# A two-layer hybrid block with eight experts on one core: who splits the first projection, products in the router's gaps, and the order of the last weight unit

## The chip, the cores and the metric

The kernel runs on one core of a Trainium2 chip. The time is device microseconds of that core for one execution of the whole program. TensorE (PE in the profile) does the matmuls, VectorE (DVE) and GpSimd (POOL) the element-wise work, ScalarE (ACT) copies, casts and activations, SyncE (SP) issues the transfers. "The clock" below is TensorE's granted clock: 1.00 is 2.4 GHz, 0.50 is 1.2 GHz.

## The reference

256 tokens of width 1024 go through two layers, all in fp32.

```
for l in range(2):
    mix = hybrid_mixer(x, ...)      # gated conv (31 taps) + chunked retention, then w_out
    x = layer_norm(ALPHA * x + mix, ln1_g[l], ln1_b[l])
    if l == 0: f = (silu(x @ w1) * (x @ w3)) @ w2           # dense, 3584 wide
    else:      # router: logits = x @ moe_router, best 2 of 8 experts, softmax of the two
               f = sum over the two experts of gate * swiglu_expert(x)
    x = layer_norm(ALPHA * x + f, ln2_g[l], ln2_b[l])
```

In `hybrid_mixer` the input projection gives two gates of 512 for the convolution (glu), then q and k, v and g of 512 each; q and k are rotated, scored against each other under a decay mask and applied to v; the conv output and the retention output go through w_out together.

## The kernel before

**Three products for one.** A fp32 matrix is held as a high part, which is the value rounded to the matmul's fast fp32 format (`fp32r`), and a low part, value minus high part. `mm3` (L150) then does high·high, high·low and low·high, one line each (L152, L153, L154). The high part is a cast on ScalarE (L107), the low part a subtraction on VectorE or on GpSimd (L108); both are in `parts`. Tiles are named `wh`/`wl` for weights, `xh`/`xl` for x, `gah`/`gal` and `gbh`/`gbl` for the gathered tokens of two experts.

**Weights** come in units of 1 MB (128x2048), in the order in which `plan` lists them, into buffers named `raw`. A unit is split in two halves of 128x1024, "first" and "second". The object `W` is this list: `take` hands out the next half and sees to it that a few more are split beyond it, `ahead(n)` only splits ahead. The place in the program at which `take` or `ahead` is called is the place at which the cast and the subtraction stand in ScalarE's, VectorE's or GpSimd's queue: there is no scheduler, each engine runs its instructions in the order in which the code writes them (`manual_schedule`), and waits at each for what it needs. Which engine subtracts is written in the unit: `gp` for GpSimd, `None` for VectorE.

**Layer 0's start.** `glu(0)` and `glu(1)` make the first two gates; after each, `fill(n)` writes n steps of the convolution into VectorE's queue (a first step on L389, then one fused multiply-add per tap on L393). `FILL[0]` begins with 12, so one step and 11 taps stand behind `glu(0)`. Then `proj()` makes q and k from units 4 and 5, both split by GpSimd.

**Between mixer and experts (layer 1).** `ln_end` normalizes 128 tokens (tile t) in two halves of 512 columns: subtract the mean and scale (L274), then multiply by the reciprocal deviation, which GpSimd computes (`rsqrt`), and add (L280). `turn_x` transposes the result on TensorE (L293), ScalarE copies it to `xf` (L294), `logits` multiplies by the router (L322, eight columns), `choose` finds the two best experts with small VectorE operations and writes `sel`. For tile 1 nothing can be done before its `sel`: five small products with a triangle of ones rank the tokens per expert (`pr`), VectorE forms `rk` and with it the four masks `P` (L743), and `gather` multiplies x by the masks in four groups of 256 columns (`pg`, L752), each split into `gah`, `gal`, `gbh`, `gbl` before the expert's first products (`ac`) can use it. `busy(n)` puts n useless 128x128 products on TensorE: 20 before the ranking, 10 behind it.

**The end.** The last unit of the last expert (`rl`, its halves are quarters 2 and 3 of the down projection) is split by half columns. The down projection's sum `y` has two halves of 512 columns, `ys0` and `ys1` are their high and low parts, `put` (L771) brings them back to token order, and the result is added to `acc`, normalized and sent in four pieces of 128x512.

Of the kernel before, what the change touches and what calls it, by code (L numbers as in the profile page):

```python
# [38 lines left out]
TAPS = (12, 11)  # L39
ASIDE = True  # L40
COLQ, W1Q = 1, 2
WARM, WARM1, WARM2 = 40, 20, 10
MOEP = {1: 0}
LATE = 4

# [27 lines left out]
def tile_hybrid(ctx: ExitStack, tc, xT_in, x_in, ws, wm, cols, lnp, gnp, router, ident_in, rot, mask_in, out):  # L73
# [25 lines left out]
    def half(h):  # L99
        return slice(512 * h, 512 * h + 512)  # L100
# [4 lines left out]
    def parts(hi, lo, src, eng=None):  # L105

        sc.copy(hi, src)  # L107
        (eng or v).tensor_tensor(lo, src, f32(hi), op=ALU.subtract)  # L108

    def split(shape, src, pool, tag, bufs=None, eng=None):  # L110
        p = pair(shape, pool, tag, bufs)
        parts(p[0], p[1], src, eng)
        return p
# [7 lines left out]
    def new_spl():  # L121
        scount[0] += 1
        return pair([128, 1024], spools[(scount[0] - 1) % len(spools)], "w")
# [22 lines left out]
    def plan(src, eng=None, kinds=("first", "second")):  # L146
        unit = src if isinstance(src, Unit) else Unit(src, eng)
        W.items += [(k, unit) for k in kinds]
# [14 lines left out]
    for l in range(DEPTH):  # L163
        b = l * MIXU
        for q in (0, 1, 4, 5, 6, 7, 2, 3, 8, 9):
            if l > 0 and q < 2:
                plan(ws[b + q], kinds=("whole",))
            else:
                plan(Unit(ws[b + q], gp if q >= POOL_GLU else None, 2 if l == 0 and q == 1 else 1))
        for q in (2, 3):  # L170
            plan(ws[b + 10 + q], kinds=("whole",))
        for q in (0, 1):
            plan(Unit(ws[b + 10 + q], gp, at=SPL if (l, q) == (DEPTH - 1, 0) else None))
        if l == 0:
            nf, d2 = DFF // 128, None
            for f in range(nf + LATE):
                if f < nf:
                    u = ws[DEPTH * MIXU + f // 2 * 3 + f % 2]
                    plan(u, kinds=("whole",) if f < 2 else ("first", "second"))
                g = f - 1 if f < nf - LATE + 1 else f - LATE  # L180
                if 0 <= g and not nf - LATE < f < nf:
                    if g % 2 == 0:
                        d2 = Unit(ws[DEPTH * MIXU + g // 2 * 3 + 2])
                    plan(d2, kinds=(("first", "second")[g % 2],))
# [83 lines left out]
    def ln_end(t, x, s, st, gt, aside=False):  # L268

        mv = sm.tile([128, 2], F32, tag="mv", name="mv")  # L270
        v.bn_aggr(mv, st)
        rs = rsqrt([128, 1], mv[:, 1:2])
        for h in range(2):
            v.scalar_tensor_tensor(s[:, half(h)], s[:, half(h)], mv[:, 0:1], gt[:, 0, half(h)],  # L274
                                   op0=ALU.subtract, op1=ALU.mult)
            if aside:
                sc.mul(s[:, half(h)], s[:, half(h)], rs[:, 0:1])
                gp.tensor_tensor(x[:, t, half(h)], s[:, half(h)], gt[:, 1, half(h)], op=ALU.add)
            else:
                v.scalar_tensor_tensor(x[:, t, half(h)], s[:, half(h)], rs[:, 0:1], gt[:, 1, half(h)],  # L280
                                       op0=ALU.mult, op1=ALU.add)
# [3 lines left out]
        nc.sync.dma_start(gt, bass.AP(tensor=lnp.tensor, offset=lnp.offset + i * 2 * D, ap=[[0, 128], [D, 2], [1, D]]))  # L285
        return gt

    def turn_x(t, psum):

        for k in range(0, KD, 4):  # L290
            p = psum.tile([128, 4, 128], F32, tag="wk", name="wk")
            for j in range(4):
                pe.transpose(p[:, j, :], x[:, t, 128 * (k + j):128 * (k + j) + 128], ident)  # L293
            sc.copy(xf[:, k:k + 4, tok(t)], p)  # L294
# [74 lines left out]
    def mixer(l, psum, mp, me, heads, then):  # L369
# [179 lines left out]
        for cc in range(2):  # L549
            glu(cc)  # L550
            if l == 0 and cc == 0:
                for q in range(W1Q, 4):
                    part_w(1, q, r1)
                nc.sync.dma_start(rott, rot)
                nc.sync.dma_start(ident, ident_in)
            fill(next(F))
        if l == 0:
            nc.sync.dma_start(mask, mask_in)
        diags()
        pq = proj()  # L560
# [49 lines left out]
        for t in range(NT):  # L610
            s, st = ln_new(mp, ("PT", "qk")[t])
            if t < NT - 1:
                for k in range(0, 4, 2):
                    for h in range(2):
                        wout_c(t, h, range(k, k + 2))
                for h in range(2):
                    ln_sum(t, h, acc[t][h], x, s, st)
            else:
                for h in range(2):
                    wout_c(t, h)  # L620
                    ln_sum(t, h, acc[t][h], x, s, st)
                turn_x(0, psum)
                if l > 0:
                    pl = bank(psum, [128, NT, NE])
                    logits(pl, 0)
                else:
                    heads = then(psum)
            ln_end(t, x, s, st, gt, ASIDE and l > 0 and t == 0)
        if l > 0:
            choose(0, pl[:, 0, :])  # L630
            parts(xn[0][:, 0, :], xn[1][:, 0, :], x[:, 0, :])
        turn_x(NT - 1, psum)
        if l == 0:
            part_x()
            W.ahead(3)
        else:
            logits(pl, 1)
            parts(xn[0][:, 1, :], xn[1][:, 1, :], x[:, 1, :])
            choose(1, pl[:, 1, :])
        return heads  # L640

# [125 lines left out]
    def put(ys, PT, t, new=None):  # L767

        p = new() if new else ptp.tile([128, 512], F32, tag="tp", name="pc")
        for i in range(2):  # L770
            pe.matmul(p, PT[:, tok(t)], ys[i], start=(i == 0), stop=(i == 1))  # L771
        return p

    def add(p, t, h, g, to=None):
        o = acc[:, t, half(h)]
        v.scalar_tensor_tensor(o if to is None else to, p, g, o, op0=ALU.mult, op1=ALU.add)  # L776
# [47 lines left out]
    def down(hT, q, w, y, first, last, hs=(0, 1)):  # L824
        for h in hs:
            mm3(y[h], two(hT, A, q), two(w, A, half(h)), first and q == 0, last and q == 3)
# [22 lines left out]
            pass  # L849

    g0 = tokens_of(0)
    W.ahead(4)
    cnt = mo.tile([128, 1], F32, name="cnt")
    v.tensor_reduce(cnt, pr[:, 2, :], axis=AX.X, op=ALU.max)
    cnti = mo.tile([128, 1], I32, name="cnti")
# [86 lines left out]
    seq[:] = raw2[:1]  # L942
    gt = load_lnp(3)
    seq[:], pools[:] = [], [raw] * RAW1
    Wl = [W.take(0), W.take(0)]
    for q in range(2):
        down(hT, q, Wl[q], y, False, False)
    Wl = [new_spl(), new_spl()]
    for h in range(2):
        for q in range(2):  # L950
            parts(Wl[q][0][:, half(h)], Wl[q][1][:, half(h)], rl[:, 1024 * q + 512 * h:1024 * q + 512 * h + 512])
    ys = []
    for h in range(2):
        for q in range(2):
            down(hT, 2 + q, Wl[q], y, False, q == 1, (h,))
        ys.append(split([128, 512], y[h], late[0], f"ys{h}"))
    sts = [sm.tile([128, 2, 6], F32, tag="st", name="st") for t in range(NT)]
    PT, gate_of = got[NE - 1][1], lambda t: gate[:, t, NE - 1:NE]
    ps = [[put(ys[h], PT, t, (None, new_ac)[h]) for t in range(NT)] for h in range(2)]
    mv = sm.tile([128, NT, 2], F32, tag="mvl", name="mvl")  # L960
    rs = sm.tile([128, NT], F32, tag="rsl", name="rsl")
    ve = sm.tile([128, NT], F32, tag="vel", name="vel")
# [1 line left out]
    def add_slow(p, t, h, g, part):  # L964
        o = acc[:, t, half(h)]
        sc.mul(part, p, g)
        gp.tensor_tensor(o, o, part, op=ALU.add)

    def stats(t, h, src=None):
        v.bn_stats(sts[t][:, h, :], acc[:, t, half(h)] if src is None else src)  # L970

    def moments(t):
        v.bn_aggr(mv[:, t, :], sts[t])
        v.tensor_scalar(ve[:, t:t + 1], mv[:, t, 1:2], EPS, None, op0=ALU.add)
        gp.tensor_tensor(rs[:, t:t + 1], ve[:, t:t + 1], neghalf[:, :1], op=ALU.pow)  # L975
# [8 lines left out]
        v.scalar_tensor_tensor(to, o, rs[:, t:t + 1], gt[:, 1, half(h)], op0=ALU.mult, op1=ALU.add)  # L984


    for h in range(2):
        add_slow(ps[h][1], 1, h, gate_of(1), raw2[3 + h].tile([128, 512], F32, tag="raw", name="part"))
    for t in range(NT):
        for h in range(2):  # L990
            if t == 0:
                add(ps[h][0], 0, h, gate_of(0), ps[h][0])
            stats(t, h, ps[h][0] if t == 0 else None)
        moments(t)

    fin = raw2[5].tile([128, NT, D], F32, tag="raw", name="fin")
    nm = sm.tile([128, 1], F32, tag="nm", name="nm")
    n0 = new_ac()
    norm1(1, 0, n0, acc[:, 1, half(0)])
    v.scalar_tensor_tensor(nm, mv[:, 1, 0:1], -1.0, rs[:, 1:2], op0=ALU.mult, op1=ALU.mult)  # L1000
    o = fin[:, 1, half(1)]
    sc.activation(o, acc[:, 1, half(1)], AF.Identity, scale=rs[:, 1:2], bias=nm[:, 0:1])
    gp.tensor_tensor(o, o, gt[:, 0, half(1)], op=ALU.mult)
    gp.tensor_tensor(o, o, gt[:, 1, half(1)], op=ALU.add)
    n = new_y()
    for h in range(2):
        norm1(0, h, n[h], ps[h][0])
        norm2(0, h, fin[:, 0, half(h)], n[h])
        send(0, h, fin[:, 0, half(h)])
    norm2(1, 0, fin[:, 1, half(0)], n0)  # L1010
    for h in range(2):
        send(1, h, fin[:, 1, half(h)])

    for h in range(2):
        sc.copy(acc[:, 0, half(h)], ps[h][0])

# [142 lines left out]
```

## Time and profile before

| | |
|---|---|
| median of 3 runs | 1452.86 us (1452.01 to 1454.47) |
| the profiled execution | 1453.59 us |
| its span, first to last instruction | 1451.8 us |
| TensorE busy | 1427.4 us (98%) |
| VectorE busy | 1211.7 us (83%) |
| ScalarE busy | 974.7 us (67%) |
| GpSimd busy | 261.8 us (18%) |
| transfers | 436.10 MB, mean 300 GB/s |
| mean granted clock | 0.993 |

A wait in the profile is idle time of an engine just ahead of an instruction, with the instruction that released it. Times in the rows count from the span's start. Instructions of one engine overlap a little at their ends, so a row's start may lie some 0.05 to 0.1 us before the end of the one ahead of it.

### The profile page before, as it was taken

Reading aid. Unit: us, or ns where it says so; the run is one execution under the profiler, and the core shown is the slowest. Engines: PE = TensorE matmul, PEld = TensorE weight load, DVE = VectorE, ACT = ScalarE, POOL = GpSimd, SP = SyncE. Lnnn points to the kernel's source line nnn. Section 1 sums busy time; section 2 is a strip of 40 time slices with the busy share of each in tenths; the row PEclk is TensorE's granted clock in tenths of the full one; section 3 lists DMA queues with packets and bytes.
Section 4 is the critical chain, followed back from the end, with each engine's and each line's share of the span. In section 5 each row is a group of like instructions: output and inputs, shape, how many; then the busy total and the mean of one; then the engine's idle time right before and its main releaser. Section 6 shows DMA issues by size and latency. Waiting matters only on the chain. (4 is left out here: it accounts for less than half of the span.)

```text
span 1451.8 us, 19734 instructions
## 1 busy us (share of the span) xinstructions
PE 1427.4 (98%) x7385; PEld 1205.5 (83%) x7385; DVE 1211.7 (83%) x1408; ACT 974.7 (67%) x1157; POOL 261.8 (18%) x136
## 2 busy tenths in 40 slices
PE   8999999999999999999999999999999999999996
PEld 8869999999867888888888888888888888888884
DVE  7966455447987989999999998999999899999997
ACT  6425444443544887877777777777777787777774
POOL 5720000001851111111111111111111111111111
PEclk9999999999998999999999999999999999999998
DMA  9536544544638799999999998999999899999951
GB/s 377 213 117 234 201 175 177 202 174 174 211 136 328 319 370 361 350 340 362 372 361 376 358 375 316 368 374 359 381 374 361 327 371 365 352 377 364 370 232 60
DMA packets 62312, 436.10 MB, mean 300 GB/s; under 512 B 7041, under 2 KB 7425, under 8 KB 9857
## 3 DMA queue, kind: packets, MB, share of 16 engines
q1 hardware_dynamic: 62208, 434.77, 78.8%
q8 instruction: 60, 0.98, 0.3%
q14 instruction: 44, 0.35, 0.1%
HBM read 433.69 MB, written 1.05 MB: 299 GB/s over the span
## 5 line engine op out<-in xcount | busy, mean ns | idle before, releaser
L108 DVE TENSOR_TENSOR wl<-raw,wh 128x1024 fp32r<-128x1024 f32 (+1 forms) x705 | 881.1, 1285 | 59.8 <-ACT wh L107 36.1
L107 ACT CAST wh<-raw 128x1024 fp32r<-128x1024 f32 (+1 forms) x802 | 822.1, 1046 | 156.5 <-PE ac L154 89.9
L108 POOL TENSOR_TENSOR wl<-raw,wh 128x1024 fp32r<-128x1024 f32 x97 | 235.0, 2440 | 1096.9 <-ACT wh L107 1005.6
L152 PE MATMUL ac<-wh,gah 128*128 128x512 f32 x448 | 177.1, 395 | 0.0
L153 PE MATMUL ac<-wl,gah 128*128 128x512 f32 x448 | 174.6, 390 | 0.5 <-POOL wl L108 0.5
L154 PE MATMUL ac<-wh,gal 128*128 128x512 f32 x448 | 174.8, 390 | 0.0
L154 PE MATMUL y<-wh,htl 128*128 128x512 f32 x448 | 174.4, 389 | 0.0
L153 PE MATMUL y<-wl,hth 128*128 128x512 f32 x440 | 171.7, 390 | 0.1
L152 PE MATMUL y<-wh,hth 128*128 128x512 f32 x440 | 171.4, 390 | 0.0
L152 PE MATMUL wk<-xh,wh 128*128 128x256 f32 x512 | 144.5, 282 | 0.6 <-ACT wh L107 0.6
L154 PE MATMUL wk<-xh,wl 128*128 128x256 f32 x512 | 143.8, 281 | 0.2 <-DVE wl L108 0.2
L153 PE MATMUL wk<-xl,wh 128*128 128x256 f32 x512 | 143.8, 281 | 0.0
L393 DVE SCALAR_TENSOR_TENSOR wk<-u,colt,wk 128x256 f32<-128x256 f32 x209 | 99.9, 488 | 5.7
L154 PEld LDWEIGHTS ac<-wh,gal 128*128 128x128 f32 x448 | 84.1, 188 | 17.9
L153 PEld LDWEIGHTS ac<-wl,gah 128*128 128x128 f32 x448 | 84.3, 188 | 17.6 <-POOL wl L108 0.9
L154 PEld LDWEIGHTS y<-wh,htl 128*128 128x128 f32 x448 | 84.1, 188 | 17.4
L154 PEld LDWEIGHTS wk<-xh,wl 128*128 128x128 f32 x512 | 98.0, 191 | 0.4 <-DVE wl L108 0.4
L153 PEld LDWEIGHTS y<-wl,hth 128*128 128x128 f32 x440 | 82.6, 188 | 18.8 <-DVE wl L108 2.0
L152 PEld LDWEIGHTS wk<-xh,wh 128*128 128x128 f32 x512 | 96.4, 188 | 2.0 <-ACT wh L107 0.8
L152 PEld LDWEIGHTS ac<-wh,gah 128*128 128x128 f32 x448 | 84.1, 188 | 16.6
L153 PEld LDWEIGHTS wk<-xl,wh 128*128 128x128 f32 x512 | 96.3, 188 | 0.9
L152 PEld LDWEIGHTS y<-wh,hth 128*128 128x128 f32 x440 | 82.7, 188 | 17.1
(217 smaller groups left out, 2024.1 us busy)
## 6 DMA issues: line engine op xcount, KB each, us to landing
raw<-in_wm_dram SPq DMA_DIRECT2D x336, 1024.0 KB, 6.8
raw<-in_ws_dram SPq DMA_DIRECT2D x68, 1024.0 KB, 4.9
raw<-in_lnp_dram SPq DMA_DIRECT2D x4, 1024.0 KB, 5.1
raw<-in_ws_dram SPq DMA_DIRECT2D x8, 256.0 KB, 5.2
xf<-in_xT_dram SPq DMA_DIRECT2D x4, 256.0 KB, 4.1
x<-in_x_dram SPq DMA_DIRECT2D x1, 1024.0 KB, 7.3
out_dram<-fin SPq DMA_DIRECT2D x4, 256.0 KB, 2.8
mask<-in_mask_dram SPq DMA_DIRECT2D x1, 768.0 KB, 12.5
```

The costliest lines, as they stand in the source:

```text
L107: sc.copy(hi, src)
L108: (eng or v).tensor_tensor(lo, src, f32(hi), op=ALU.subtract)
L152: pe.matmul(o, a[0], b[0], start=first, stop=False, skip_group_check=True)
L153: pe.matmul(o, a[0], b[1], start=False, stop=False, skip_group_check=True)
L154: pe.matmul(o, a[1], b[0], start=False, stop=last, skip_group_check=True)
L393: v.scalar_tensor_tensor(d, u[:, cc, k:k + S], w[:, k:k + 1], o, op0=ALU.mult, op1=ALU.add)
```

## The change

The diff has five parts. In layer 0 the first half of unit 4, the first that `proj()` uses, is subtracted by VectorE instead of GpSimd, and the transfers of `rott` and `ident` (128 and 64 KB) are issued behind three weight units instead of ahead of them. `ln_end` writes both halves' L274 before the two of L280. In layer 1 `turn_x` gets 4, 5 and 2 useless products in front of three of its four groups of transposes. The low part of x of tile 1 is no longer written ahead of `choose(1)` but behind the masks `P`, and the `W.ahead(4)` that stood there is gone. At the end all four quarters of the down projection are done for the first half of the columns, then for the second, and the two `put` of the first half stand ahead of the second half's last quarter.

```
-WARM, WARM1, WARM2 = 40, 20, 10
+WARM, WARM0, WARM1, WARM2 = 40, ((0, 4), (5, 2)), 20, 10
...
-                plan(Unit(ws[b + q], gp if q >= POOL_GLU else None, 2 if l == 0 and q == 1 else 1))
+                plan(Unit(ws[b + q], (None, gp) if (l, q) == (0, 4) else gp if q >= POOL_GLU else None))
...
         for h in range(2):
             v.scalar_tensor_tensor(s[:, half(h)], s[:, half(h)], mv[:, 0:1], gt[:, 0, half(h)],
                                    op0=ALU.subtract, op1=ALU.mult)
+        for h in range(2):
             if aside:
...
-    def turn_x(t, psum):
+    def turn_x(t, psum, warm=(0, 0), w=None):
 
         for k in range(0, KD, 4):
+            if warm[k // 4]:
+                busy(warm[k // 4], w)
...
-                nc.sync.dma_start(rott, rot)
-                nc.sync.dma_start(ident, ident_in)
             fill(next(F))
         if l == 0:
+            nc.sync.dma_start(ident, ident_in)
+            nc.sync.dma_start(rott, rot)
             nc.sync.dma_start(mask, mask_in)
...
             logits(pl, 1)
-            parts(xn[0][:, 1, :], xn[1][:, 1, :], x[:, 1, :])
+            sc.copy(xn[0][:, 1, :], x[:, 1, :])
             choose(1, pl[:, 1, :])
...
     g0 = tokens_of(0)
-    W.ahead(4)
+    v.tensor_tensor(xn[1][:, 1, :], x[:, 1, :], f32(xn[0][:, 1, :]), op=ALU.subtract)
...
+    def first_half():
+        ps.append([put(ys[0], PT, t) for t in range(NT)])
+        for t in range(NT):
+            add(ps[0][t], t, 0, gate_of(t), ps[0][t])
+            stats(t, 0, ps[0][t])
+
     for h in range(2):
-        add_slow(ps[h][1], 1, h, gate_of(1), raw2[3 + h].tile([128, 512], F32, tag="raw", name="part"))
...
+        for q in range(4):
+            down(hT, q, Wl[q], y, False, q == 3, (h,))
+            if h and q == 2:
+                first_half()
+        ys.append(split([128, 512], y[h], late[0], f"ys{h}"))
+    ps.append([put(ys[1], PT, t, new_ac) for t in range(NT)])
+    add(ps[1][0], 0, 1, gate_of(0), ps[1][0])
+    add_slow(ps[1][1], 1, 1, gate_of(1), raw2[3].tile([128, 512], F32, tag="raw", name="part"))
+    stats(0, 1, ps[1][0])
+    moments(0)
+    stats(1, 1)
+    moments(1)
```

VectorE's queue at layer 0's start, before the change; `u` is a gate times its sigmoid, `wl` of 128x512 belongs to the second gate's unit, the lines with `colt` are the convolution:

```order
L423 TENSOR_TENSOR u<-wk,sgl 128x256
L108 TENSOR_TENSOR wl<-raw,wh 128x512 x2
L389 TENSOR_SCALAR wk<-u,colt 128x256
L393 SCALAR_TENSOR_TENSOR wk<-u,colt,wk 128x256 x11
L423 TENSOR_TENSOR u<-wk,sgl 128x256
```

The same place in the changed kernel:

```order
L426 TENSOR_TENSOR u<-wk,sgl 128x256
L108 TENSOR_TENSOR wl<-raw,wh 128x512 x2
L392 TENSOR_SCALAR wk<-u,colt 128x256
L396 SCALAR_TENSOR_TENSOR wk<-u,colt,wk 128x256 x11
L108 TENSOR_TENSOR wl<-raw,wh 128x1024
L426 TENSOR_TENSOR u<-wk,sgl 128x256
```

The one new instruction, the split of unit 4's first half, stands behind the 11 taps and ahead of the second gate.

VectorE's queue from the end of `choose(1)` to the third group of gathered tokens, before; `wl` are here halves of the first expert's second unit:

```order
L318 TENSOR_TENSOR sel<-s_148,s_149 128x8
L732 SCALAR_TENSOR_TENSOR rk<-pr,sel 128x16
L743 TENSOR_SCALAR P<-iota,rk 128x128 x4
L108 TENSOR_TENSOR wl<-raw,wh 128x1024 x2
L854 TENSOR_REDUCE cnt<-pr 128x1
L856 CAST cnti<-cnt 128x1
L108 TENSOR_TENSOR gal<-pg,gah 128x256
L108 TENSOR_TENSOR gbl<-pg,gbh 128x256
L108 TENSOR_TENSOR gal<-pg,gah 128x256
L108 TENSOR_TENSOR gbl<-pg,gbh 128x256
L108 TENSOR_TENSOR gal<-pg,gah 128x256
```

The same place in the changed kernel:

```order
L321 TENSOR_TENSOR sel<-s_148,s_149 128x8
L736 SCALAR_TENSOR_TENSOR rk<-pr,sel 128x16
L747 TENSOR_SCALAR P<-iota,rk 128x128 x4
L856 TENSOR_TENSOR xl<-x,xh 128x1024
L858 TENSOR_REDUCE cnt<-pr 128x1
L860 CAST cnti<-cnt 128x1
L108 TENSOR_TENSOR gal<-pg,gah 128x256
L108 TENSOR_TENSOR gbl<-pg,gbh 128x256
L108 TENSOR_TENSOR gal<-pg,gah 128x256
L108 TENSOR_TENSOR gbl<-pg,gbh 128x256
L108 TENSOR_TENSOR wl<-raw,wh 128x1024 x2
L108 TENSOR_TENSOR gal<-pg,gah 128x256
```

One `xl` takes the place of the two `wl` behind the masks, and the two `wl` now stand between the second and the third group; their casts on ScalarE moved with them, from ahead of the first `gah` to ahead of the third.

VectorE's queue at the end, before; `pc` and `ac` are results of `put`, `st` statistics of the norm:

```order
L108 TENSOR_TENSOR ys0l<-y,ys0h 128x512
L108 TENSOR_TENSOR ys1l<-y,ys1h 128x512
L776 SCALAR_TENSOR_TENSOR pc<-pc,gate,acc 128x512
L970 BN_STATS st<-pc 128x6
L776 SCALAR_TENSOR_TENSOR ac<-ac,gate,acc 128x512
L970 BN_STATS st<-ac 128x6
```

The same place in the changed kernel:

```order
L108 TENSOR_TENSOR ys0l<-y,ys0h 128x512
L780 SCALAR_TENSOR_TENSOR pc<-pc,gate,acc 128x512
L966 BN_STATS st<-pc 128x6
L780 SCALAR_TENSOR_TENSOR pc<-pc,gate,acc 128x512
L966 BN_STATS st<-pc 128x6
L108 TENSOR_TENSOR ys1l<-y,ys1h 128x512
L780 SCALAR_TENSOR_TENSOR ac<-ac,gate,acc 128x512
L966 BN_STATS st<-ac 128x6
```

Four operations on the first half now stand ahead of the split `ys1l` of the second.

## Rows read from the trace of the kernel before

**Rows 1.** Waits of TensorE: us in total, times, longest.
```profile
PE wk L153 <- POOL wl L108: 1.9, 1, 1.9
```

**Rows 2.** Busy time by stretch; the last: TensorE alone, then clock, DMA share, GB/s.
```profile
700.00:1400.00 700.00, 699.68 (x3192) 578.90 (x3192) 643.31 (x585) 550.88 (x596) 100.43 (x41) 1.00 0.96 364
...
449.00:449.50 0.50, 0.36 (x3) 0.91 0.90 377
...
459.60:460.00 0.40, 0.40 (x5) 0.94 1.03 430
```

**Rows 3.** Instructions in order of time (start, duration), layer 0's start.
```profile
0.99 4.45 PE L328 MATMUL wk<-ones 128*128 128x128 bf16 x40 [0.99 <-POOL ones L199]
...
15.41 5.74 DVE L393 SCALAR_TENSOR_TENSOR wk<-u,colt,wk 128x256 f32<-128x256 f32 x11
16.86 2.00 ACT L107 CAST wh<-raw 128x1024 fp32r<-128x1024 f32 x2 [2.75 <-DMA raw<-in_ws_dram]
18.00 2.36 POOL L108 TENSOR_TENSOR wl<-raw,wh 128x1024 fp32r<-128x1024 f32 x1 [16.16 <-ACT wh L107]
20.41 0.50 PE L153 MATMUL wk<-wl,xh 128*128 128x512 f32 x1 [1.85 <-POOL wl L108]
21.06 0.42 DVE L423 TENSOR_TENSOR u<-wk,sgl 128x256 f32<-128x256 f32 x1
```

**Rows 4.** GB/s by slice of 36 us, from the page.
```profile
GB/s 377 213 117 234 201 175 177 202 174 174 211 136 328 319 370 361 350 340 362 372 361 376 358 375 316 368 374 359 381 374 361 327 371 365 352 377 364 370 232 60
```

**Rows 5.** Instructions in order of time, a place where GpSimd and VectorE split at once.
```profile
475.66 2.74 POOL L108 TENSOR_TENSOR wl<-raw,wh 128x1024 fp32r<-128x1024 f32 x1 [24.94 <-ACT wh L107]
477.04 2.44 DVE L108 TENSOR_TENSOR wl<-raw,wh 128x1024 fp32r<-128x1024 f32 x1 [0.25 <-ACT wh L107]
```

**Rows 6.** Instructions in order of time, from the second norm to the choice.
```profile
446.80 1.90 PE L322 MATMUL wk<-rt,xf 128*128 128x8 f32 x16
448.33 0.75 DVE L280 SCALAR_TENSOR_TENSOR x<-s,rs,raw 128x512 f32<-128x512 f32 x1 [0.44 <-POOL rs L252]
450.59 1.11 PE L293 MATMUL wk<-ident,x 128*128 128x128 f32 x4 [0.55 <-DVE x L280]
451.68 3.56 PE L322 MATMUL wk<-rt,xf 128*128 128x8 f32 x16
452.57 2.35 DVE L108 TENSOR_TENSOR xl<-x,xh 128x1024 fp32r<-128x1024 f32 x2
455.27 0.17 DVE L308 TENSOR_REDUCE m<-wk 128x1 f32<-128x8 f32 x1 [0.35 <-PE wk L322]
```

**Rows 7.** Instructions in order of time, from the masks to the experts' first products.
```profile
453.17 1.99 ACT L107 CAST wh<-raw 128x1024 fp32r<-128x1024 f32 x2
458.81 2.35 DVE L108 TENSOR_TENSOR wl<-raw,wh 128x1024 fp32r<-128x1024 f32 x2
464.89 0.37 ACT L107 CAST gah<-pg 128x256 fp32r<-128x256 f32 x1 [1.10 <-PE pg L752]
466.15 0.42 DVE L108 TENSOR_TENSOR gbl<-pg,gbh 128x256 fp32r<-128x256 f32 x1 [0.44 <-ACT gbh L107]
469.32 0.40 PE L154 MATMUL ac<-wh,gal 128*128 128x512 f32 x1
```

**Rows 8.** Instructions in order of time, the end.
```profile
1429.98 1.22 DVE L108 TENSOR_TENSOR wl<-raw,wh 128x1024 fp32r<-128x1024 f32 x1
1435.50 0.40 PE L771 MATMUL pc<-ys0h,PTx 128*128 128x512 f32 x1
1436.51 0.40 PE L771 MATMUL ac<-ys1h,PTx 128*128 128x512 f32 x1
1436.93 0.75 DVE L776 SCALAR_TENSOR_TENSOR pc<-pc,gate,acc 128x512 f32<-128x512 f32 x1
1437.47 2.62 POOL L967 TENSOR_TENSOR acc<-acc,part 128x512 f32<-128x512 f32 x2 [22.47 <-ACT part L966]
1445.45 1.27 POOL L1004 TENSOR_TENSOR fin<-fin,raw 128x512 f32<-128x512 f32 x1
```

More of the change, by code (lines that the diff above doesn't have):

```diff
@@ L621, in mixer @@
                     ln_sum(t, h, acc[t][h], x, s, st)
-                turn_x(0, psum)
+                wb = bank(psum, [128, 512]) if l > 0 else None
+                turn_x(0, psum, WARM0[0] if l > 0 else (0, 0), wb)
                 if l > 0:
@@ L631, in mixer @@
             parts(xn[0][:, 0, :], xn[1][:, 0, :], x[:, 0, :])
-        turn_x(NT - 1, psum)
+        turn_x(NT - 1, psum, WARM0[1] if l > 0 else (0, 0), wb)
         if l == 0:
@@ L944, in tile_hybrid @@
     seq[:], pools[:] = [], [raw] * RAW1
[L945 to L948, printed above, removed]
+    Wl = [W.take(0), W.take(0), new_spl(), new_spl()]
     for h in range(2):
         for q in range(2):
[L951 to L956, printed above, removed]
+            parts(Wl[2 + q][0][:, half(h)], Wl[2 + q][1][:, half(h)], rl[:, 1024 * q + 512 * h:1024 * q + 512 * h + 512])
     sts = [sm.tile([128, 2, 6], F32, tag="st", name="st") for t in range(NT)]
     PT, gate_of = got[NE - 1][1], lambda t: gate[:, t, NE - 1:NE]
-    ps = [[put(ys[h], PT, t, (None, new_ac)[h]) for t in range(NT)] for h in range(2)]
+    ys, ps = [], []
     mv = sm.tile([128, NT, 2], F32, tag="mvl", name="mvl")
@@ L984, in norm2, with norm @@
         v.scalar_tensor_tensor(to, o, rs[:, t:t + 1], gt[:, 1, half(h)], op0=ALU.mult, op1=ALU.add)
-    for h in range(2):
-        add_slow(ps[h][1], 1, h, gate_of(1), raw2[3 + h].tile([128, 512], F32, tag="raw", name="part"))
[L989 to L994, printed above, removed]
+    def first_half():
[3 more added lines that the diff above has]
+            stats(t, 0, ps[0][t])
+    for h in range(2):
+        for q in range(4):
[10 more added lines that the diff above has]
+    moments(1)
     fin = raw2[5].tile([128, NT, D], F32, tag="raw", name="fin")
     nm = sm.tile([128, 1], F32, tag="nm", name="nm")
-    n0 = new_ac()
-    norm1(1, 0, n0, acc[:, 1, half(0)])
+    n = new_y() + [new_ac()]
+    def norm(i, t, h):
+        norm1(t, h, n[i], ps[h][t])
+        norm2(t, h, fin[:, t, half(h)], n[i])
+        send(t, h, fin[:, t, half(h)])
+    norm(0, 0, 0)
     v.scalar_tensor_tensor(nm, mv[:, 1, 0:1], -1.0, rs[:, 1:2], op0=ALU.mult, op1=ALU.mult)
@@ L1004, in tile_hybrid @@
     gp.tensor_tensor(o, o, gt[:, 1, half(1)], op=ALU.add)
[L1005 to L1015, printed above, removed]
+    norm(1, 0, 1)
+    norm(2, 1, 0)
+    send(1, 1, o)
+    for t, h in ((0, 0), (0, 1), (1, 0)):
+        sc.copy(acc[:, t, half(h)], ps[h][t])
     if GENERAL:
```

## The prediction

> **What bounds the kernel now.** I looked first at busy time by stretch: between 700 and 1400 us TensorE is busy 699.68 of 700 us [rows 2], so the expert phase is a solid run of products, and a stall ahead of it or work behind it is added to the time in full. Then at TensorE's waits: the longest is 1.9 us for a low part from GpSimd, once [rows 1]. Then at four stretches in order of time: layer 0's start, the turn into the experts, their first products, and the end. The clock is at its upper level, 2.4 GHz, nearly throughout. It falls at 449.46 and is back at about 459.6 [rows 2], with TensorE doing little in between.
>
> **First projection: the split goes to VectorE.** Now: the casts of unit 4 begin at 16.86, as soon as its transfer lets them; GpSimd subtracts from 18.00 to 20.36; TensorE, idle for 1.85 us, goes on at 20.41 [rows 3]. VectorE's queue is strict: the new split stands behind 11 taps, which run from 15.41 to 21.15, and the next instruction after them began at 21.06 [rows 3]. A split alone on VectorE costs 1.18 (two in 2.35) [rows 7], so without any obstacle it ends at 22.3, and TensorE goes on at about 22.4: later by 2.0. That is the lower end. That the split could start with its cast is excluded by the queue.
>
> The obstacle is GpSimd, which still splits the other halves. At 475.66 it took 2.74 for such a split, to 478.40, and VectorE's, begun at 477.04, took 2.44 in place of 1.18 [rows 5]: 1.3 us of it had passed when GpSimd ended, and what was left is a whole split. The one that comes second waits for all of the other. The Trainium skill, "SBUF — State Buffer", section "Who interferes with whom", says this as a rule: a VectorE instruction with two SBUF inputs and a GpSimd instruction that reads SBUF hold a shared port in turn, each for a whole instruction. The trace agrees (2.44).
>
> So it counts who is first. Unit 4's second half is cast by 18.86, GpSimd takes 2.36, so it is at it until about 21.3. The two tables, 192 KB, now move behind the weights; at the 377 GB/s of the first slice [rows 4] that is 0.5 us, by which unit 4 and 5 land earlier, since the cast waited for the transfer [rows 3]. Then GpSimd is through at about 20.8, 0.3 us ahead of VectorE, and takes its next half until 23.2. VectorE's split then ends at 24.4: later by 4.0, the upper end. Both ends are close (0.3 us decide); I take 4.0, as its inputs are rows. The wait is not given back: from 20.41 on TensorE had what it needed, and VectorE, behind it, moves with it. The earlier transfers gain nothing else, as the split is behind the taps.
>
> **The clock there.** TensorE, idle for 1.85 us, kept its clock; now it is idle for 3.9 to 5.9. If the clock falls, the products behind it run at 1.2 GHz for a while. Sixteen router products take 3.56 at that level and 1.90 at the upper [rows 6], so 47% of such a time is lost; at the program's start the 40 useless products took 4.45 us, all at the lower rate (111 ns each) [rows 3]. A return of that size costs at most 4.45 × 0.47 = 2.1; a clock that holds, nothing. I take 1.4. The Trainium skill, "TensorE: Matmul & The Clock Gate", section "HAM oscillation — how this bites in real kernels", ties a fall to a long idle gap. By that alone nothing would fall in the router, where the longest gap is 0.55 [rows 6]; there the trace differs, and the rows decide: router products, eight columns wide, did not hold it.
>
> **Norm and router.** The second subtraction fills the 0.44 us in which VectorE waited for GpSimd [rows 6]: the second half of x comes some 0.5 earlier, the first 0.2 later. In the two other norms (layer 0's mixer, the dense part) TensorE has a head of gated products to do, so this is worth nothing there. Now logits(1) ends only at 455.24 (16 products at half rate) and `choose(1)` starts at 455.27 [rows 6]. With the clock as before logits would end 0.2 earlier. With the clock kept they take 1.90 in place of 3.56 and their transposes shrink too; then VectorE is the limit: `choose(0)` ends at 452.57 - 0.5, one split of x (1.18) follows, not two [rows 6], and `choose(1)` starts at about 453.2: 2.0 earlier. Eleven products add some 0.6 us at the upper rate.
>
> **Masks to first products.** Counted from the masks' end, 458.8 now [rows 7]: one x split (1.18) takes the place of two weight splits (2.35), so the first pair `ga`, `gb` can end some 0.8 earlier, but TensorE's fourth gather product waits for this split. The two casts (1.99) and splits (2.35) that were made while ScalarE was idle, at 453.17 [rows 7], now stand ahead of the third pair. A pair takes 1.68 (464.89 to 466.57); two of them, overlapped, end 4.9 after the masks; the splits end at 7.9, the third pair at 9.1, where it was 7.7. Behind it another cast and split and the fourth pair, whose `gal` comes 11.3 after the masks. The last group's first product with a `gal`, at 469.32, was at 10.4 [rows 7]. So 0.9 is lost, with a following wait some 1.0 (0.5 to 1.3). The stretch as a whole: clock as before +0.8; kept -1.0; kept over the logits, then lost in the idle time while `choose(1)` runs (the 20 useless products need only some 1.1 us at the upper rate and end 1.8 us ahead of `sel`), so that the gather runs slowly (+0.6): -0.4. I take the last: the gaps are filled where the clock fell, but the new gap is longer than they were.
>
> **The end.** The first half's sum is ready 1.0 earlier. The second's comes 1.4 later: four `put` products (1435.50 to 1436.51, 1.0) stand ahead of its last three, and the second quarter's low part, ready at 1431.2, holds the faster first half up by 0.4 [rows 8]. `ys1l`, behind it, now waits for four operations on the first half and ends at 1439.4, where the same four began after it, at 1436.93 [rows 8]. What follows has only one column half left for each tile, and GpSimd one addition in place of two (2.62) [rows 8], so 0.7 comes back; but VectorE has six norm operations behind the moments where one of them was done in a wait. Step by step GpSimd's last addition, now 1445.45 to 1446.72 [rows 8], ends at 1448.7: 2.0 later. The sends are less crowded, so that the last lands 0.8 to 1.6 later; I take 1.0.
>
> **Sum.** 4.0 + 1.4 - 0.4 + 1.0 = 6.0. On the profiled execution that is 1453.59 + 6.0 = 1459.6. Its time lies 0.7 above the median of the runs shown, so for a median I forecast 1452.86 + 6.0 = 1458.9. Some 0.2%, 2.9 us, is what can be told from no change.
>
> **Rivals.**
> 1. VectorE is first at the port. It takes the place of 4.0 by 2.1, with TensorE idle for 3.9 us. For it: GpSimd's end is 0.3 us from VectorE's arrival. With the clock lost 4.1 in all, 1457.0; with the clock kept 2.1 - 0.4 + 1.0 = 2.7, 1455.6, not slower by what can be told. It decides whether GpSimd's second split ends after 21.1.
> 2. The clock holds everywhere, with VectorE first at the port: 2.1 - 1.0 + 1.0 = 2.1, 1455.0. For it: 1.85 us of idleness did no harm; against it: 10 us at the lower level where no gap was over 0.55 [rows 2, 6].
> 3. The split doesn't come late at all, as the taps would be through earlier: TensorE's 1.85 us vanish, less 0.6 for the cast and split themselves: -1.3 - 0.4 + 1.0 = -0.7, 1452.2. It needs a start before 19.1; against it stand 11 taps in the queue.
> 4. All bounds at their far end: 4.0 + 2.1 + 0.8 + 1.6 = 8.5, 1461.4.
>
> **How the numbers follow.** Forecast 0.45, slower. Rival 1 0.23, of which two thirds slower. Rival 2 0.12 and rival 3 0.08, same. Rival 4 0.05, slower. Left over 0.07, faster, for something that I don't see. Slower 0.65, same 0.28, faster 0.07. The range leaves out rivals 3 and 4 and what is left over, 0.2: 1453.8 to 1460.6. The forecast's own is 1457.2 to 1460.6.
>
> **What would show it.** TensorE's first `wl` of the projection at 24.4 (22.4 by rival 1), and a VectorE split of over 2 us there; half the granted clock behind it. `choose(1)` 2 us earlier relative to the mixer's last product, but the fourth pair's `gal` 11 us behind the masks. At the end `ys1l` 2.4 later relative to the last unit's first product, GpSimd's last addition 2.0. The prediction is wrong if the split stands alone at 21.1 and the clock stays, or if the first half's earlier start carries through to the last send.

## The result and the profile after

The changed kernel takes 1460.96 us (median of 5 runs, 1459.6 to 1462.01), the kernel before 1452.86 in its 5 runs: a ratio of 1.0055, 95% interval 1.0044 to 1.0066, so slower by 8.1 us (6.4 to 9.6). Forecast were 1458.9 and a range from 1453.8 to 1460.6. The direction was right; the time lies just above the range. The profiled execution took 1459.6 us, with a span of 1457.8; against the profiled 1453.59 of before that is +6.0, exactly the sum forecast. That agreement is luck: the experiments show why two single executions could not carry it.

TensorE's waits now (us in total, times, longest):

```profile
PE wk L153 <- DVE wl L108: 4.3, 1, 4.3
...
PE ac L775 <- DVE ys1l L108: 1.2, 1, 1.2
PE pr L730 <- DVE sel L321: 1.2, 1, 1.2
```

The 1.9 us of [rows 1] became 4.3, with VectorE in GpSimd's place. The wait for `sel` is new, and the one for `ys1l` was 0.2 us before. In order of time:

```profile
14.55 2.00 ACT L107 CAST wh<-raw 128x1024 fp32r<-128x1024 f32 x2 [0.60 <-DMA raw<-in_ws_dram]
16.64 8.07 POOL L108 TENSOR_TENSOR wl<-raw,wh 128x1024 fp32r<-128x1024 f32 x3 [14.80 <-ACT wh L107]
17.78 0.39 PE L152 MATMUL wk<-wh,xh 128*128 128x512 f32 x1
20.90 1.56 DVE L108 TENSOR_TENSOR wl<-raw,wh 128x1024 fp32r<-128x1024 f32 x1
22.52 0.79 PE L153 MATMUL wk<-wl,xh 128*128 128x512 f32 x1 [4.35 <-DVE wl L108]
...
449.39 0.60 PE L296 MATMUL wk<-ident,x 128*128 128x128 f32 x4
...
455.22 1.92 PE L325 MATMUL wk<-rt,xf 128*128 128x8 f32 x16 [0.43 <-DVE rl L319]
...
459.51 0.17 PE L730 MATMUL pr<-sel,tri 128*128 128x8 bf16 x1 [1.23 <-DVE sel L321]
...
469.70 0.42 DVE L108 TENSOR_TENSOR gal<-pg,gah 128x256 fp32r<-128x256 f32 x1
...
1443.14 0.67 DVE L108 TENSOR_TENSOR ys1l<-y,ys1h 128x512 fp32r<-128x512 f32 x1
1443.87 0.50 PE L775 MATMUL ac<-ys1l,PTx 128*128 128x512 f32 x1 [1.23 <-DVE ys1l L108]
...
1452.04 1.27 POOL L1017 TENSOR_TENSOR fin<-fin,raw 128x512 f32<-128x512 f32 x1
```

The split stands behind the taps and ends at 22.46; TensorE goes on at 22.52, where it went on at 20.41 [rows 3]. The second logits take 1.92 us, not 3.56 [rows 6], and then TensorE idles for 1.23 us until `sel`. The third pair's `gal` comes behind two weight splits. At the end `ys1l` waits for four operations on the first half, and GpSimd's last addition ends at 1453.31, not at 1446.72 [rows 8].

Busy time by stretch, for TensorE, its weight loads, VectorE, ScalarE and GpSimd; the three numbers at the end are granted clock, DMA share and GB/s:

```profile
22.00:24.00 2.00, 1.48 (x4) 1.19 (x5) 1.93 (x5) 2.00 (x8) 2.00 (x1) 0.50 1.00 417
...
28.00:30.00 2.00, 2.00 (x10) 1.64 (x9) 1.88 (x4) 0.66 (x1) 2.00 (x2) 0.98 0.98 410
...
456.00:458.00 2.00, 2.00 (x29) 2.00 (x29) 1.86 (x6) 0.36 (x1) 0.00 (x0) 1.00 1.07 451
458.00:460.00 2.00, 0.78 (x15) 0.70 (x13) 1.42 (x8) 0.00 (x0) 0.00 (x0) 0.54 0.98 410
```

Two falls of the clock matter. Behind the longer wait the products run at 1.2 GHz until about 28, and the clock that held over the logits falls at 458.2, behind the useless products and just as the idle time begins.

### The profile page after: what moved, and what is told of

It is laid out like the page before. It is cut to its first block, busy times and chain, and to the rows that moved or that the text cites. A ratio compares the mean times of both kernels' runs of the same rounds, so it can differ in the third digit from the quotient of the medians.

```text
span 1457.8 us, 19758 instructions
## 1 busy us (share of the span) xinstructions
PE 1428.9 (98%) x7396; PEld 1204.7 (83%) x7396; DVE 1213.8 (83%) x1410; ACT 974.5 (67%) x1157; POOL 259.9 (18%) x134
```

## The experiments

Every profile below is divided at two places: tile 0's transposes in the router's norm (449.39 above, 445.19 before) and an expert's transposes some 260 us later (`ph`, at 710.99 in the changed kernel, 706.62 before). That gives three stretches: the front, the router with the first products, and the rest. In each diff only the lines that matter are shown.

**GpSimd's split back, transfers moved.**

```
-  (None, gp) if (l, q) == (0, 4) else gp if q >= POOL_GLU else None
+  gp if q >= POOL_GLU else None
```

> The changed kernel with the first half of unit 4 given back to GpSimd; the tables' transfers stay behind the weights. Theory T (the loss is the split's place: 2.1 us of longer wait, and 2.6 us because the clock falls in it): unit 4 lands 2.3 us earlier than before the change, so GpSimd subtracts from some 15.7 to 18.0 and the product of the low part waits for under 0.4 us; the clock stays up and the first projection is 6 to 6.5 us ahead of the changed kernel's. With the end (+1.7) and the router (+0.2) kept: 0.2 us or so below the kernel before, 1452.5 to 1454.5. Rival R1 (the transfers' new order is what costs: the tables come late, or GpSimd's splits crowd): no gain, 1459 to 1461. Rival R2 (the excess of the median lies in other places of the program, where the clock falls): 1455 to 1457.

Measured: 1453.98 us (11 runs), ratio to before 1.0007 (0.9998 to 1.0016). Theory T's number, and about 7 us less than the changed kernel. TensorE hardly waits:

```profile
16.13 4.75 POOL L108 TENSOR_TENSOR wl<-raw,wh 128x1024 fp32r<-128x1024 f32 x2 [14.29 <-ACT wh L107]
...
18.58 0.50 PE L153 MATMUL wk<-wl,xh 128*128 128x512 f32 x1
```

So who splits the first half carries most of the loss. But the total agreed in part by luck: in the profile the front (443.35) came 1.84 us ahead of the one profile of the kernel before that was at hand (445.19), and the router's stretch took 263.20 us instead of 261.43.

**VectorE's split ahead of the taps.**

```
                     part_w(1, q, r1)
+                W.ahead(3)
             fill(next(F))
```

> The changed kernel with VectorE's split of unit 4's first half moved from behind the 11 taps to ahead of the convolution's first step. Theory T: VectorE waits for the cast (done at 15.6), splits by some 17.0, and the taps start 1.7 us later; the product of the low part, wanted at 18.2, waits for nothing, the clock stays up, and 4.3 us or more of the shift go, as in the kernel with GpSimd: 1452.5 to 1455. The second gate u comes 0.5 to 1 us later, which TensorE doesn't wait for. Rival R1 (VectorE is short of time there, so that what is put ahead of the taps comes back as a later wait for u or for the rotation's tables): 1457 to 1460.

Measured: 1454.98 us, ratio 1.0014 (1.0005 to 1.0023).

```profile
16.12 1.23 DVE L108 TENSOR_TENSOR wl<-raw,wh 128x1024 fp32r<-128x1024 f32 x1 [0.89 <-ACT wh L107]
...
17.84 5.74 DVE L396 SCALAR_TENSOR_TENSOR wk<-u,colt,wk 128x256 f32<-128x256 f32 x11
...
73.51 1.25 PE L502 MATMUL wk<-ident,rz 128*128 128x128 f32 x8 [0.67 <-DVE rz L590]
```

It is the place behind the taps, not VectorE as such: the low part's product starts at 18.48 without a wait. The delay that VectorE takes on here comes back in part, as 0.67 us of waiting for `rz` at 73.5, and the front ends at 444.23, 0.9 us behind the first experiment's.

**The clock held through the wait.** 70 useless products between the first product and the one that waits (`ps[2]` is one more bank):

```
+  pe.matmul(p, X[0][:, 0, tok(0)], w[0][:, 0, :], start=True, stop=False, skip_group_check=True)
+  busy(held, ps[2])
+  pe.matmul(p, X[0][:, 0, tok(0)], w[1][:, 0, :], start=False, stop=False, skip_group_check=True)
```

> The changed kernel with 70 useless 128x128 products on TensorE between the first projection's first product and the one that waits for the low part (some 3.9 us of its 4.35 us of waiting), one more PSUM bank for them. It prices the fall of the clock by itself: the wait stays 4.3 us (busy now), the split still ends at 22.4. Theory T: the clock stays up, the 13 products behind take 0.21 us each and not 0.43, and the time falls by 2.2 to 2.6 us against the changed kernel, to 1458.2 to 1459. Rival R1 (the slow products hid work that then becomes the next wait): the shift at 56 us stays at 4.2 and the time at 1460 to 1461. Rival R3 (the products' clock falls in any case): the same, with the granted clock at half behind 22.5.

Measured: 1458.38 us (ratio 1.0044, 1.003 to 1.0058), 3.6 less than the changed kernel in the same job.

```profile
18.64 0.40 PE L440 MATMUL wk<-wh,xh 128*128 128x512 f32 x1
18.88 4.08 PE L331 MATMUL wk<-ones 128*128 128x128 bf16 x70
22.90 0.50 PE L442 MATMUL wk<-wl,xh 128*128 128x512 f32 x1
23.23 0.39 PE L443 MATMUL wk<-wh,xl 128*128 128x512 f32 x1
23.46 0.40 PE L152 MATMUL wk<-wh,xh 128*128 128x512 f32 x1
```

The low part comes no earlier (22.90), but the products behind it are 0.23 us apart, not 0.43, and the front ends at 447.26, 1.9 to 2.95 ahead of the changed kernel's 449.39, 450.21 and 449.18 (the last two below). In this profile the clock stays up from the wait to the router: with the idle time filled it does not fall there. So the fall in the changed kernel comes from the idle time and costs that much.

**The changed kernel again**, for a second profile.

> The changed kernel as it is, for a second profile: where in the program do executions of it that take longer lose their clock? Theory T: the profiled execution had the fewest windows at half clock (mean clock 0.991), and one with 0.989 or 0.990 shows one or two more stretches of 2 to 10 us at half clock, at places where TensorE is idle or does small products, worth 1 to 2.5 us. Rival R2: the time differs without the clock, by transfers that land later and TensorE waiting for them.

Measured: 1461.95 us (1460.86 to 1465.47), ratio 1.0070 (1.0057 to 1.0084). The first wait is 4.39 us again; the router differs:

```profile
454.00:456.00 2.00, 1.71 (x11) 1.56 (x10) 1.83 (x8) 0.58 (x1) 0.12 (x1) 0.63 1.04 434
...
460.00:462.00 2.00, 1.85 (x22) 1.79 (x20) 1.57 (x9) 0.00 (x0) 0.00 (x0) 0.50 0.99 410
...
466.00:468.00 2.00, 2.00 (x10) 1.90 (x10) 0.85 (x2) 1.09 (x3) 0.00 (x0) 0.50 1.03 430
```

Here the clock falls ahead of the second logits, at 454.5, and stays down past the gather, to 468.2: 263.18 us for the stretch, not 261.60. Theory T holds for most of it: of the 2.3 us between the two profiled spans the router gives 1.6 and the front 0.8. The useless products keep the clock over the second logits in one execution and not in another.

**The transfers alone**, in the kernel before: the two tables' transfers of the diff are moved, and who splits what stays as it was.

> The kernel before with one part of the change alone: the transfers of the two tables moved behind three weight units. Theory T: the parts add up. The first projection gains what it gained in the kernel with GpSimd's split (1.84 us at tile 0's transposes), the router and the end are those of before: 1451 us, 1450.7 to 1451.5. Rival R1 (the change's router makes up part of that gain, or the earlier front only moves the wait to the router): 1452.3 to 1453.

Measured: 1452.58 us, ratio 0.9995 (0.9986 to 1.0004). That is rival R1's number. Theory T's 1451 was not met, though the profiled execution took 1451.69 with the front at 443.26. Either the front's gain is lost elsewhere, or the front of the kernel before was unusual in its one profile; four further profiles below show the second (445.19 was the latest of five, with a mean of 444.4).

**The end of before**, in the first experiment's kernel.

> The changed kernel with GpSimd's split as in the first experiment, and the end as before the change (the last unit quarter by quarter, put behind it). Theory T: the end of the change costs 1.5 to 1.7 us from the last unit's first product on, so 1.55 us less than the first experiment's 1454.0: 1452.0 to 1452.8. Rival R4 (the end's length is set by the transfers out and the drain of the program, and only moves with the execution): 1453.5 to 1454.5.

Measured: 1453.07 us, ratio 0.9997 (0.9988 to 1.0006), between the two theories; by the ratios 1.5 us less than the first experiment, each with an uncertainty of 1.3. The profile decides for theory T: from `ph` to the span's end 745.2 us, as in the kernel before; 746.7 to 746.8 in each of the eight profiles with the change's end.

**Without the useless products**, in the first experiment's kernel: `WARM0 = ((0, 0), (0, 0))`.

> The first experiment without the 11 useless products in front of the transposes. Theory T: they keep the clock over the second logits in a few executions only; the rest of the router's change (x's second low part behind the masks, the weights' splits behind the second pair) costs some 0.8 to 1.8 us when the clock is down over both logits and gather. Without the useless products the clock falls as it did before the change: the router takes 0.8 us more than before, 0 to 1 us less than in the first experiment: 1453 to 1454. Rival R5 (the useless products do hold the clock in most executions): 1454.5 to 1456.

Measured: 1454.37 us, ratio 1.0007 (0.9998 to 1.0016), the same as with them and between the two theories. The router took 262.20 us with the clock down from 448.0 to 458.3, over the second logits. What they are worth in most executions can't be told from this.

**x's part and the splits back in their order**, in the first experiment's kernel.

```
-  sc.copy(xn[0][:, 1, :], x[:, 1, :])
+  parts(xn[0][:, 1, :], xn[1][:, 1, :], x[:, 1, :])
...
-  v.tensor_tensor(xn[1][:, 1, :], x[:, 1, :], f32(xn[0][:, 1, :]), op=ALU.subtract)
+  W.ahead(4)
```

> The first experiment with x's second low part ahead of the second choice again and the weights' splits (ahead of the gather) put back; the useless products and the norm's order stay. Theory T: the loss of 0.8 to 1.8 us between tile 0's transposes and the experts is the later splits; with them back the stretch takes what it took before the change (261.4 us to the transposes at 706.6) or less: 1452.3 to 1453.2. Rival R6 (the loss is the clock, which the useless products shift to a worse place): no gain, 1453.7 to 1454.7.

Measured: 1453.99 us, ratio 1.0005 (0.9996 to 1.0014): no gain in the median, rival R6's number; theory T's was missed. The profiled execution kept the clock over the logits:

```profile
451.02 1.92 PE L325 MATMUL wk<-rt,xf 128*128 128x8 f32 x16 [0.43 <-DVE rl L319]
...
456.43 0.17 PE L730 MATMUL pr<-sel,tri 128*128 128x8 bf16 x1 [2.35 <-DVE sel L321]
```

Its stretch took 261.01 us, against 261.60 in the changed kernel's profile with the clock kept over the same place: in like conditions the change's order costs 0.6, less than the clock moves the stretch.

**What helped, together**: the kernel before with the transfers moved, the useless products and the norm's order.

> A version put together from what helped: the kernel before with the tables' transfers moved, the 11 useless products and the norm's order; x's second low part, the weights' splits and the end as before the change. Theory T: the first projection gives 1.8 to 1.9 us, the end nothing, and the router's stretch (443.3 to 704.7 in the kernel with the tables alone, 261.4 us) takes 261.0 where the clock is kept over the second logits and up to 262.5 where it falls ahead of them: 1451.2 in the good case, 1452 to 1453 as a median, no more than 0.5 us from the kernel with the tables alone. Rival R5 (useless products hold the clock in most executions): 1451.0 to 1451.5 as a median.

Measured: 1450.93 us, ratio 0.9985 (0.9976 to 0.9994): faster than both kernels, if only by 0.15% against the one before, and below the medians of theory T and rival R5. Eight of 11 runs took 1450.25 to 1451.00, three 1452.51 to 1453.37; the profiled one was one of the three (1452.64, stretch 262.31). Which part gives what stays open: the transfers alone gave 0.9995 with an interval that meets this one.

**The router's idle times filled further**, in that kernel.

```
-WARM, WARM0, WARM1, WARM2 = 40, ((0, 4), (5, 2)), 20, 10
+WARM, WARM0, WARM1, WARM2 = 40, ((0, 8), (0, 6)), 42, 10
...
         for k in range(KD):
+            if w is not None:
+                busy(1, w)
```

> The same with the router's idle times filled further: 8 useless products before tile 0's second transposes, one before each of the first logits' products, 6 before tile 1's second transposes, 42 in place of 20 while the second choice runs. Theory T (the clock falls where TensorE idles or does eight-column products): it stays up from the mixer to the experts, the second logits take 1.9 us, the gather's products 0.21 us apart are 0.11 apart; the stretch takes some 259.0 to 260.3 us, in every execution, and the time is 1449.5 to 1451. Rival R7 (the clock falls all the same, or the products delay what they stand ahead of): 1451.5 to 1453.5, half the clock in some windows between 443 and 462.

Measured: 1452.14 us, ratio 0.9990 (0.9981 to 0.9999). The clock stayed up over both logits and the choice, to 455.95, and fell while the gather's first products ran, 2 us behind one idle time and ahead of another:

```profile
453.94 0.17 PE L732 MATMUL pr<-sel,tri 128*128 128x8 bf16 x1 [1.13 <-DVE sel L321]
...
457.70 0.58 PE L758 MATMUL pg<-P,xh 128*128 128x256 f32 x1 [1.05 <-DVE cnt L860]
```

Rival R7. With the logits fast, the second choice waits for VectorE's two splits of x, so TensorE still idles. The stretch took 262.56 us: the gather and the first products now run at half the clock, and the further useless products may cost time themselves; what each costs was not separated. Three of 11 runs took 1450.2 to 1450.4; whether the clock stayed up in them isn't shown, as none of them was profiled.

**The split alone**, in the kernel before: unit 4's first half goes to VectorE, and the tables' transfers stay as they were.

> The kernel before with one part of the change alone: unit 4's first half split by VectorE, the tables' transfers as they were. It puts the step of the prediction on the first projection to the test with the unit landing as late as before (cast at 16.9). The prediction's step (VectorE comes second at the port, GpSimd's next split in front of it): VectorE's split takes 2.2 us or more and ends at 24.4, TensorE waits 5.9 us, clock down behind it: before + 6 to 6.6, 1459 to 1460. Theory T (the port is yielded early, the taps alone decide): the split takes 1.2 to 1.6 us and ends at 22.4 to 22.8, the wait is 4.2 us and the clock falls: before + 4.3 to 4.8, 1457.2 to 1458.2. Rival R8 (the clock holds): before + 2.1, 1455.

Measured: 1457.82 us, ratio 1.0035 (1.0021 to 1.0049).

```profile
17.45 12.72 POOL L108 TENSOR_TENSOR wl<-raw,wh 128x1024 fp32r<-128x1024 f32 x5 [15.61 <-ACT wh L107]
...
21.00 2.20 DVE L108 TENSOR_TENSOR wl<-raw,wh 128x1024 fp32r<-128x1024 f32 x1
...
23.26 0.79 PE L153 MATMUL wk<-wl,xh 128*128 128x512 f32 x1 [4.99 <-DVE wl L108]
```

The time is theory T's, the split between the two theories: it takes 2.20 us, nearly the prediction's 2.44, and the wait is 4.99. The unit did not land as late as the expectation assumed; its cast began at 15.36, not at 16.9. The router (261.44) and the rest (745.2) are those of before, so the whole loss is in the front, 449.10.

**The kernel before again**, four more profiles, and a third of the changed kernel.

> The kernel before as it is, for a second profile: is its clock as changeable? Theory T: the router's stretch, from tile 0's transposes to the expert's transposes at 706, takes 261.4 us in the profile already read; if other executions lose the clock elsewhere in it, it takes 261 to 262.5, less spread than the changed kernel's 261.6 to 263.3, as the clock falls at the second logits and is back before the gather. Rival R2: the same stretch within 0.1 us, and the time's spread comes from another place.

> The kernel before, a third profile. Theory U (formed on the second profile of it): the 1.85 us for which TensorE waits for the first low part of unit 4 in the profile that the prediction used is not usual; the transfer landed late there (cast after 2.75 us of waiting, 1.2 to 1.3 in two others with the tables ahead). Usual is a wait of 0.4 to 0.8 us, tile 0's transposes at 443.3 to 443.8, and a router stretch of 262 to 263 us. Against that, the change costs 6 us or more in the first projection, not 4.2. Theory V (the first profile was usual, the second not): a wait of 1.6 to 2.0 us, transposes at 445.0 to 445.4.

> The kernel before, a fourth profile; as for the third: by theory U a wait of 0.4 to 0.8 us at the first low part and transposes at 443.3 to 443.8, by theory V 1.6 to 2.0 and 445.0 to 445.4.

> The kernel before, a fifth profile; as for the third: by theory U a wait of 0.4 to 0.8 us at the first low part and transposes at 443.3 to 443.8, by theory V 1.6 to 2.0 and 445.0 to 445.4.

> The changed kernel, a third profile. Theory U: the split behind the taps doesn't depend on when the unit lands, so TensorE's wait is 4.3 to 4.4 us again, transposes at 449.4 to 450.3, the router's stretch 261.6 to 263.2, the end 746.7: a time of 1459.5 to 1462. Theory V: the wait varies by over 1 us here too.

Times: 1453.36 us as the median of 8 runs (ratio 0.9997, 0.9987 to 1.0007); then single runs of 1452.89, 1452.03 and 1453.53; the changed kernel 1460.03. The first low part in the second, third and fourth profile of before:

```profile
19.05 0.51 PE L153 MATMUL wk<-wl,xh 128*128 128x512 f32 x1 [0.59 <-POOL wl L108]
```

```profile
20.11 0.50 PE L153 MATMUL wk<-wl,xh 128*128 128x512 f32 x1 [1.30 <-POOL wl L108]
```

```profile
19.32 0.51 PE L153 MATMUL wk<-wl,xh 128*128 128x512 f32 x1 [0.49 <-POOL wl L108]
```

In the fifth it waits for nothing, since a slow clock at 9 to 12 us had made TensorE itself late (20.39). Neither U nor V is right: the wait has no usual size, and 1.85 us [rows 3] was the longest of five. The kernel before's clock is changeable too: in the second profile it fell twice in the router (449.5 to 456.3 and 459.7 to 463.1), and the stretch took 262.99 us, more than theory T's 261 to 262.5. The changed kernel's third profile waits 3.88 us, with the low part at 22.84: by U the wait was to be 4.3 to 4.4. Its second logits are slow:

```profile
22.84 0.74 PE L153 MATMUL wk<-wl,xh 128*128 128x512 f32 x1 [3.88 <-DVE wl L108]
...
449.18 0.60 PE L296 MATMUL wk<-ident,x 128*128 128x128 f32 x4
...
455.24 3.42 PE L325 MATMUL wk<-rt,xf 128*128 128x8 f32 x16
...
711.41 0.60 PE L822 MATMUL ph<-ident,hh 128*128 128x128 f32 x4
```

By stretch, in us:

| | front | router | rest |
|---|---|---|---|
| before, five profiles | 445.19, 443.46, 444.47, 443.72, 445.06 | 261.43, 262.99, 261.42, 261.41, 261.39 | 745.1 to 745.4 |
| changed, three profiles | 449.39, 450.21, 449.18 | 261.60, 263.18, 262.23 | 746.7 to 746.8 |
| difference of means | +5.2 | +0.6 | +1.5 |

The sum is 7.3, within the measured interval of 6.4 to 9.6; what is left to 8.1 is within what these profiles and runs can tell. The pair of executions that was compared first joined the latest front of before to the shortest router of the changed kernel: 4.2 + 0.2 + 1.6 = 6.0.

## Why the prediction was wrong in size

**First projection: the port's order was wrong, and the sum came out by luck.** Forecast 4.0 + 1.4, measured 5.2. In the two executions that were compared first, the low part comes at 22.52 and 20.41 [rows 3]: a delay of 2.1, not 4.0. That is the delay of the rival with VectorE first at the port, and this rival's condition came true: GpSimd's second split ended at 21.38, behind 21.1. The prediction had GpSimd through at 20.8 and at its next split when VectorE came. But unit 4 landed 2.3 us earlier, not 0.5 (cast at 14.55, where it was 16.86), so at 20.90 GpSimd was still at the second of its splits. VectorE waited for what was left of that one and went ahead of the third: 1.3 to 1.6 us instead of 2.44. The Trainium skill, "SBUF — State Buffer", section "Who interferes with whom", says that the later of the two waits out the other's whole instruction. The traces agree, and they show that only what is left of it counts: what was left of GpSimd's running split when VectorE's began was 0.22, 0.48, 0.52, 1.12 and 1.36 us (the changed kernel's third, first and second profile, the split alone, [rows 5]), and VectorE's took 1.31, 1.56, 1.60, 2.20 and 2.44, each time 1.08 or 1.09 more.

Two things made up for the 4.0. The wait of before is usually shorter: the low part comes at 19.86 on average of its five profiles and at 22.82 in the changed kernel's three, 3.0 apart. And the slow clock, put at 1.4 and at most 2.1, costs 2.2: from the low part to tile 0's transposes it is 424.4 to 424.8 us in the five profiles of before and 424.4 with the idle time filled, but 426.3 to 427.1 in the changed kernel. Some 13 products stand 0.43 us apart in its first profile, where 0.23 is the upper rate.

**Router: the step that failed.** "Kept over the logits, then lost in the idle time", at -0.4, was chosen over "clock as before +0.8"; measured +0.6 in the means of the table. The mechanism was right for the execution in the first profile: logits in 1.92, `choose(1)` at 457.25 (2.2 earlier in relation to the transposes), the gather at half the clock; only the fall came ahead of the idle time and not in it. But it was so in one execution of the changed kernel's three, and in one of seven profiles with this order and the useless products; even there the stretch was 0.2 longer than before. What the order costs is seen where the clock behaves alike. In nine profiles it fell 3.1 to 4.2 us behind tile 0's transposes and stayed down for 10.2 us: the stretch took 262.20 to 262.25 us in the four with the new order (the changed kernel's third, VectorE's split ahead of the taps, the held clock, without useless products) and 261.39 to 261.44 in the five with the old one (four of the kernel before, the split alone). That is +0.8, the bound that was left. Three profiles with the new order and 13.7 us of the lower clock took 263.18 to 263.29. The chain behind the masks was right: in the changed kernel's third profile, where the clock is up again from 463.3, the two weight splits end 7.9 us behind the masks, the third pair 9.1 and the fourth `gal` 11.2 (forecast 7.9, 9.1 and 11.3). In the first, with the gather at half the clock, each came some 1.0 later. The gain to set against this was not reliable. The fall of before, read as 449.46, is at 449.41 by the 0.91 of [rows 2], which changes nothing.

**End: mis-sized.** Forecast 1.0, measured 1.5. GpSimd's last addition is 2.25 later in relation to the last unit's low parts (forecast 2.0), and the sends gave back 0.6 to 0.7 of it, not 1.0.

**The carry-over.** The forecast took the sum from one execution to the median by a constant (0.7). The front of that execution was the latest of five and made the loss look 0.8 smaller; no single profile could say so. Against the forecast's 6.0 the table's sum is 7.3: the router lies 1.0 above its term, the end 0.5, and the front 0.2 below.

Of the rivals, the one with VectorE first at the port was right on the port and, for the two executions compared, on the delay; its 1457.0 fell short because the slow clock, the router and the end cost more and the wait of before is usually shorter. The one in which the clock holds everywhere had the same delay but is refuted by the slow products behind the wait in all three profiles, and the one in which the split doesn't come late by waits of 3.9 to 4.4 us. With all bounds at their far end the forecast was 8.5 us, near the measured 8.1; of its terms the clock's 2.1, the router's 0.8 and the end's 1.6 are close to what was measured, and only the 4.0 is not.

## What to carry to other kernels

A subtraction moved to a less busy engine belongs where that engine's queue is empty when its input comes: behind 11 taps it cost the front 5 us against the kernel before, ahead of them 0.9 against GpSimd's split. A stall of TensorE of 3.9 us or more ahead of dense products was paid twice, once as idle time and once at half the clock; in the kernel before, waits of up to 1.85 us left the clock up. Before summing terms of 1 us from a single profile, look at a second execution: in the kernel before, the front moved by 1.7 us from one execution to another and the router by 1.6.

## What the hardware showed that was not expected

In each of the 18 profiles the clock fell in the router, but the same instructions meet the fall at different places: in the changed kernel's router 8.8 us behind tile 0's transposes in one execution, 4.3 in another and 3.8 in the third; the half clock lasted 6.8, 13.7 and 10.2 us. Useless products put the fall off in some executions and removed it in none: with them it came 3.7 to 13.3 us behind the transposes, without them 3.1 to 6.3. The Trainium skill, "TensorE: Matmul & The Clock Gate", section "HAM oscillation — how this bites in real kernels", ties such falls to idle gaps: the one in the first projection, and its absence when 70 products filled it, agree; the router's fall in the second profile, with no gap over 0.3 us behind tile 0's transposes, does not.

How soon a unit lands also varied: ScalarE waited for unit 4's transfer for 1.13 to 2.75 us with the 192 KB of tables ahead of it (five profiles) and for 0.36 to 0.62 with them behind (ten), where the clock was up at the start.
